# The conv projection as seven products of blocks, with its sums on VectorE

## The chip, the cores and the metric

The kernel runs on one NeuronCore of a Trainium2 chip. Its time is device microseconds of one execution; of several executions the median is taken. The engines of the core are TensorE (PE; its weight loads are listed apart as PEld), VectorE (DVE), ScalarE (ACT), GpSimd (POOL) and SyncE (SP), which issues most of the DMA transfers.

## The reference

One decoder layer on x of 1024 tokens x 1024 channels, float32. What matters here is the middle of it:

```python
a = rms_norm(a, subln_w[l]) * (1.0 - lam_init)
y_a = a.reshape(B, S, ATTN_WIDTH) @ w_proj_attn[l]

u_a, u_b = jnp.split(u, 2, axis=-1)
c = causal_depthwise_conv(u_a * jax.nn.sigmoid(u_b), conv_w[l], conv_b[l])
c = jax.nn.silu(layer_norm(c, conv_ln_w[l], conv_ln_b[l]))
y_b = c @ w_proj_conv[l]

g_a, g_b = jnp.split(jax.nn.sigmoid(g + gate_b[l]), 2, axis=-1)
x = x + (g_a * y_a + g_b * y_b) @ w_out[l]

h = rms_norm(x, ffn_norm_w[l])
gt, up = jnp.split(h @ w_gate_up[l], 2, axis=-1)
x = x + (jax.nn.silu(gt) * up) @ w_down[l]
```

All matrices of the middle part are 1024 x 1024. Below, c is the normed conv branch, m the gated sum g_a * y_a + g_b * y_b.

## The kernel before

Every large product is made of float32r matmuls. An operand is split into a part hi (a cast on ACT, split_hi, line 119) and a rest lo (a subtraction on DVE, split_lo, line 124), and mm3 (line 152) adds hi·hi, hi·lo and lo·hi into one PSUM bank, so that each product of 128 x 128 by 128 x 512 is three matmuls.

The stages follow one another: the input projection, interleaved with the conv taps and the attention of eight heads; then the attention projection y_a, the conv projection y_b, the output projection, and the feed-forward part. Up to the attention projection TensorE's operand is h, transposed, in two SBUF tiles of 128 x 8 x 1024 (hT_hi and hT_lo, tags xhi and xlo of the pool "big"). The same two places then hold cT_hi and cT_lo, then h2_hi and h2_lo, so that each waits until the one before it has been read for the last time.

**Attention projection** (lines 1486 to 1506). Two column blocks of w_proj_attn run together, then six one by one; each is 2 token halves x 8 k x 3 matmuls into two banks. ya_out loads the gate (gated, line 1469: a DMA and a Tanh on ACT, tag gt, four tiles), multiplies on DVE (gate_twice) and stores y_a's gated part in DRAM (ya_d). Beside it runs the conv branch's layer norm, as a generator per token half (ln_chunks, line 1396) that is advanced in steps given by two lists (lines 1450 and 1458): the rows of c are loaded into the place of cT_lo; the mean comes from a matmul with the sum over channels; the differences d are squared on ACT and added on DVE; then each row is scaled, goes through Silu, and is split into cT_hi and cT_lo.

**Conv projection** (lines 1508 to 1536). Eight column blocks in groups of three, two, two and one; for each group both token halves; each is gemm_T (line 375), 8 k x 3 matmuls into one bank. Then DVE multiplies with the gate and adds the reloaded y_a part, which gives a half row of m. Three quarters of m are split for TensorE. block_sums (line 1512) makes four sums of the blocks of m on DVE and stores them in DRAM (mso).

**Output projection** (lines 1628 to 1662). It is already done as seven products of 512 x 512 blocks (Winograd's form of Strassen's method): the list WO (line 446) names for each product a block or a sum of blocks of m ("12", "S1"), a block or a sum of w_out ("T2", made early and kept in DRAM), the group of four PSUM banks into which it is added ("a", "b", "c"), and the block of the result that is read out of them after it. s_load (line 1595) reloads a sum of m from mso, and splits it. Group b lies in the pool pw, the others in the pool ps. The rows of x are loaded into tiles xa, whose room is that of the gate tiles of the stage before (pool b1, closed at line 1537). In the last product the second norm begins (norm2, line 1571), whose transposes go through banks of ps (tr_first, line 1588).

Weights come through a Stream (line 342) that loads and splits two ahead of the one that is used: 512 KB each into one of two tiles wraw, split into one of three pairs whi and wlo. What a queue's instructions follow each other in is set by a planner that simulates the program; in_order (line 205) and after (line 127) fix some orders by hand.

## Time and profile before

| what | us |
|---|---|
| median of three executions | 1740.07 |
| lowest and highest | 1739.8, 1740.08 |
| the profiled execution's own time | 1738.13 |
| its span, first to last instruction | 1736.3 |
| attention projection, from and to | 835 to 927 |
| conv projection | 927 to 1014 |
| output projection | 1014 to 1095 |

The span is what the profile covers; the execution's own time has 1.8 us more around it. Stages are given by the first matmuls of each, in us from the start of the span. In the rows of groups, a line gives the source line, the engine, the operation, the tile written and the tiles read, the count, and then busy time and mean duration, and the idle time of the engine before these instructions with what ended it. A matmul's duration in such a row is not its price: the next one starts before it ends.

### The profile page before, as it was taken

The numbers are of one execution on the slowest core, as the hardware profiler recorded it, in microseconds if no ns is written. First come the engines' busy times: TensorE is split into PE (matmuls) and PEld (weight loads), VectorE is DVE, ScalarE is ACT, GpSimd is POOL, SyncE is SP. The second block draws the span as 40 slices with busy tenths as digits, with TensorE's granted clock in tenths as the row PEclk, the third lists the DMA queues.
The fourth block names the chain that finished last, engine by engine and source line by source line (L and its number), as shares of the span: only waits on it lengthen the run. The fifth ranks groups of instructions, "written<-read, shape, count | busy, mean of one in ns | idle before, by whom it ended". The sixth has DMA issues, their size and how long they took to land.

```text
span 1736.3 us, 25111 instructions
## 1 busy us (share of the span) xinstructions
PE 1726.8 (99%) x8954; PEld 1471.5 (85%) x8954; DVE 1292.2 (74%) x2202; ACT 794.8 (46%) x1873; POOL 27.1 (2%) x101
## 2 busy tenths in 40 slices
PE   9999999999999999999999999999999999999999
PEld 6878898999999998988888888888888888888887
DVE  8689988989889898885675567976676666565554
ACT  6121141667767776754564234633333333333332
POOL 0010000000000000000000000000000000000000
PEclk9999999999999999999999999999999999999999
DMA  7269545244444345364874677235445444697663
GB/s 244 91 201 305 183 124 136 71 120 131 122 142 114 89 120 151 87 173 139 288 245 134 200 246 251 86 107 178 152 159 172 158 149 152 224 352 241 218 216 131
DMA packets 260537, 295.22 MB, mean 170 GB/s; under 512 B 17730, under 2 KB 167283, under 8 KB 260412
## 3 DMA queue, kind: packets, MB, share of 16 engines
q1 hardware_dynamic: 257676, 283.73, 50.8%
q0 software_dynamic: 2432, 9.10, 2.2%
q8 instruction: 70, 1.15, 0.3%
q10 hardware_dynamic: 304, 0.79, 0.1%
q14 instruction: 55, 0.45, 0.1%
HBM read 189.19 MB, written 90.21 MB: 161 GB/s over the span
## 4 chain that ended last, share of the span: by engine, by line
PE 95%; DVE 2%; ACT 1%; DMA 1%; issue 0%; SPq 0%; DVEq 0%
PE acc L1819 22%; PE pg L153 14%; PE pg L154 14%; PE pg L155 14%; PE acc L532 12%; PE pg L737 4%; PE wo L1641 3%; PE sc L1152 2%; PE sc L1151 2%; PE pT L1187 2%; PE pW L155 1%; PE pW L153 1%; PE pW L154 1%; PE pQ L821 1%; DMA xa<-in_x_dram 0%; PE tr L1579 0%
## 5 line engine op out<-in xcount | busy, mean ns | idle before, releaser
L610 DVE SCALAR_TENSOR_TENSOR acc<-u,cw,acc 128x1024 f32<-128x1024 f32 x240 | 306.9, 1279 | 2.6
L153 PE MATMUL pg<-hT_hi,whi 128*128 128x512 f32 x512 | 201.5, 394 | 1.2 <-ACT sgg L646 0.9
L154 PE MATMUL pg<-hT_lo,whi 128*128 128x512 f32 x512 | 201.1, 393 | 0.0
L155 PE MATMUL pg<-hT_hi,wlo 128*128 128x512 f32 x512 | 200.8, 392 | 0.0
L120 ACT CAST whi<-wraw 128x1024 fp32r<-128x1024 f32 x101 | 106.3, 1052 | 149.0 <-PE pg L154 96.4
L125 DVE TENSOR_TENSOR wlo<-draw,whi 128x1024 fp32r<-128x1024 f32 x75 | 91.8, 1224 | 89.1 <-ACT whi L120 81.5
L125 DVE TENSOR_TENSOR wlo<-wraw,whi 128x1024 fp32r<-128x1024 f32 x102 | 124.3, 1219 | 44.7 <-ACT whi L120 41.4
L153 PE MATMUL pg<-whi,hT_hi 128*128 128x256 f32 x512 | 146.1, 285 | 0.3 <-ACT jk L805 0.3
L154 PE MATMUL pg<-wlo,hT_hi 128*128 128x256 f32 x512 | 145.7, 285 | 0.0
L155 PE MATMUL pg<-whi,hT_lo 128*128 128x256 f32 x512 | 145.3, 284 | 0.0
L120 ACT CAST whi<-draw 128x1024 fp32r<-128x1024 f32 x75 | 79.1, 1055 | 129.5 <-PE acc L532 119.3
L532 PE MATMUL acc<-wlo,whi 128*128 128x512 f32 x308 | 119.8, 389 | 0.0
L532 PE MATMUL acc<-whi,wlo 128*128 128x512 f32 x308 | 119.8, 389 | 0.0
L153 PEld LDWEIGHTS pg<-hT_hi,whi 128*128 128x128 f32 x512 | 96.2, 188 | 21.3 <-ACT sgg L646 1.7
L154 PEld LDWEIGHTS pg<-hT_lo,whi 128*128 128x128 f32 x512 | 96.2, 188 | 19.4 <-issue 0.6
L155 PEld LDWEIGHTS pg<-hT_hi,wlo 128*128 128x128 f32 x512 | 96.2, 188 | 19.2
L1158 ACT ACTIVATE E<-E,mn 128x256 f32<-128x256 f32 (+7 forms) x128 | 99.4, 778 | 28.2 <-DVE mn L1153 27.9
L153 PEld LDWEIGHTS pg<-whi,hT_hi 128*128 128x128 f32 x512 | 97.6, 191 | 1.9 <-ACT jk L805 0.5
L154 PEld LDWEIGHTS pg<-wlo,hT_hi 128*128 128x128 f32 x512 | 97.6, 191 | 1.5
L155 PEld LDWEIGHTS pg<-whi,hT_lo 128*128 128x128 f32 x512 | 97.6, 191 | 0.7
L1819 PE MATMUL acc<-h_hi,whi 128*128 128x512 f32 x240 | 93.4, 389 | 0.0
L1819 PE MATMUL acc<-h_lo,whi 128*128 128x512 f32 x240 | 93.4, 389 | 0.0
(321 smaller groups left out, 4182.2 us busy)
## 6 DMA issues: line engine op xcount, KB each, us to landing
wraw<-in_w_gate_up_dram SPq DMA_DIRECT2D x44, 512.0 KB, 4.6
wraw<-in_w_in_dram SPq DMA_DIRECT2D x37, 512.0 KB, 5.4
qs<-qs SPq DMA_DIRECT2D x96, 128.0 KB, 2.3
wd<-in_w_down_dram SPq DMA_DIRECT2D x44, 256.0 KB, 3.2
tdT<-wd SPq DMA_DIRECT2D x88, 128.0 KB, 4.2
draw<-sdS SPq DMA_DIRECT2D x44, 256.0 KB
draw<-tdT SPq DMA_DIRECT2D x44, 256.0 KB, 4.3
wraw<-in_w_in_dram SPq DMA_DIRECT2D x32, 256.0 KB, 4.6
```

The costliest lines, as they stand in the source:

```text
L120: act.copy(dst, src)
L125: last_lo[0] = dve.tensor_tensor(dst, src, f32(hi), op=ALU.subtract).ins
L153: pe.matmul(o, lh, rh, start=start, stop=False)
L154: pe.matmul(o, lh, rl, start=False, stop=False)
L155: last_mm[0] = pe.matmul(o, ll, rh, start=False, stop=stop).ins
L532: m = pe.matmul(o[s_][i][:], l_[:, ts], r_[:, 512:], start=start and j + y_ == 0, stop=j == n - 1 and y_ == 2, skip_group_check=not start,)
L610: dve.scalar_tensor_tensor(acc[0][:], us[c][:, t : t + S], cw[:, c, t : t + 1], acc[0][:], op0=ALU.mult, op1=ALU.add)
L737: last_mm[0] = pe.matmul(o[:], l_, r_, start=first and n_ == 0, stop=last and n_ == len(terms) - 1).ins
L1151: pe.matmul(o[:, :w], qh[:, qs], k, start=True, stop=False)
L1158: act.activation(e[:, :nk], e[:, :nk], AF.Exp, bias=mn[:, j : j + 1], scale=-1.0, accum_out=l[:, j : j + 1])
L1641: last_mm[0] = pe.matmul(o[s_][i][:], l_, r_[:, k, :], start=start and g + k + y_ == 0, stop=g == 1 and k == 1 and y_ == 2, skip_group_che ...
L1819: pe.matmul(o[:], a_[x_][:, k, :], b_[y_][:, k, :], start=start and k + x_ + y_ == 0, stop=k == 3 and x_ == 1, skip_group_check=not start,)
```

## The change

The conv projection is done in the way of the output projection: seven products of 512 x 512 blocks, transposed. The stationary operands are blocks and sums of blocks of w_proj_conv (YO's first entry), the moving ones blocks of c and sums of them (T1 to T4).

- side_weights makes S1 to S4 of the weights in four pieces, during the attention projection's third to sixth column block, and stores them in DRAM (wps). ld_side loads a block or such a sum.
- The layer norm stores the finished rows of the first token half in DRAM too (z_d). In the second half, four rows at a time (channel blocks j and j + 4 of both token halves) give the four sums; t_split splits them into tiles that take the places of aT, once the attention projection has read these.
- The tiles of h, c, and of the second norm are cut into quarters (class Quad: channel half and token half), each a tile with its own tag.
- The seven products' partial results are kept in SBUF (part_) or added to PSUM; m's quarters are kept in SBUF (mf, in places of c), and m's sums are made there and split in place. mso and s_load are gone.
- The output projection takes S1 second; its group b is now in ps and group c in pw, and the transposes of the second norm go through pw.

The diff, cut to its core:

```diff
+class Quad:
+    def __init__(self, pool, name, tag, halves=None):
+        self.t = {
+            q: pool.tile([P, NKT // 2, 512], F32R, tag=f"{tag}{q[0]}{q[1]}", name=f"{name}{q[0]}{q[1]}")
+            for q in (halves or ((0, 0), (1, 0), (0, 1), (1, 1)))
+        }
...
-    hT_hi = big.tile([P, NKT, S], F32R, tag="xhi", name="hT_hi")
-    hT_lo = big.tile([P, NKT, S], F32R, tag="xlo", name="hT_lo")
+    hT_hi = Quad(big, "hT_hi", "xh")
+    hT_lo = Quad(big, "hT_lo", "xl")
...
-    mso = {z: [dr.tile([P, 512], F32, name=f"mso{z}_{j}") for j in range(4)] for z in ("S1", "S2", "S3", "S4")}
+    wps = {z: [dr.tile([P, 512], F32, name=f"wps{z}_{j}") for j in range(4)] for z in ("S1", "S2", "S3", "S4")}
+    z_d = [dr.tile([P, 512], F32, name=f"z_d{c}") for c in range(NKT)]
...
     WO = (
         ("12", (1, 0), "a", (0, 0), False),
+        ("S1", "T1", "c", (1, 1), False),
         ("11", (0, 0), "b", (0, 0), True),
         ("S2", "T2", "b", (0, 1), False),
-        ("S1", "T1", "c", (1, 1), False),
         ("S4", (1, 1), "c", (0, 1), True),
         ("S3", "T3", "b", (1, 1), True),
         ("22", "T4", "b", (1, 0), True),
     )
+    YO = (
+        ("12", (1, 0), "a", (((0, 0), False),)),
+        ("11", (0, 0), "b", (((0, 0), True),)),
+        ("S4", (1, 1), "c", (((0, 1), False),)),
+        ("S2", "T2", "b", (((0, 1), False),)),
+        ("S1", "T1", "d", (((1, 1), False), ((0, 1), True))),
+        ("S3", "T3", "b", (((1, 1), True),)),
+        ("22", "T4", "b", (((1, 0), True),)),
+    )
+    def ld_side(a_, g):
+        def go():
+            raw = wraw()
+            r4 = raw[:].rearrange("p (q k c) -> p q k c", k=4, c=P)
+            for q in range(2):
+                j = 2 * g + q
+                if a_ in wps:
+                    nc.sync.dma_start(raw[:, 512 * q : 512 * (q + 1)], wps[a_][j][:])
+                else:
+                    c, e = 2 * j + 2 - int(a_[0]), int(a_[1]) - 1
+                    nc.sync.dma_start(
+                        r4[:, q], wpc[512 * e : 512 * (e + 1), c * P : (c + 1) * P].rearrange("(k p) c -> p k c", p=P)
+                    )
+            return [t_[:].rearrange("p (q k c) -> p q k c", k=4, c=P) for t_ in wsplit(raw)]
...
+    ws.plan([ld_side(a_, g) for a_, _, _, _ in YO for g in range(2)])
...
-    cT_hi = big.tile([P, NKT, S], F32R, tag="xhi", name="cT_hi")
-    cT_lo = big.tile([P, NKT, S], F32R, tag="xlo", name="cT_lo")
+    cT_hi = Quad(big, "cT_hi", "xh", ((0, 0), (1, 0), (1, 1)))
+    cT_lo = Quad(big, "cT_lo", "xl")
+    LNR = []
+    TOK = (slice(0, 512), slice(512, 1024))
+    TK = {"T2": (1, 3), "T1": (5, 7), "T3": (0, 2), "T4": (4, 6)}
+    TC = {}
+    def t_split(j, sums_):
+        for z, t_ in sums_.items():
+            hi, lo = [d_[TK[z][j // 2]][:, TOK[j % 2]] for d_ in TC[z]]
+            split_hi(hi, t_[:])
+            split_lo(lo, t_[:], hi)
...
+        if sb:
+            room = big.tile([P, 4, 512], F32, tag="xh01", name="ln_d")
+            LNR.append(room)
         for c in range(NKT):
             q = half("sq") if c else s2
-            d = half("csg" if sb == 0 and c % 2 else "d")
-            dve.tensor_tensor(d[:], cc[c], mean[:], op=ALU.subtract)
-            act.activation(q[:], d[:], AF.Square)
-            nc.sync.dma_start(cc[c], d[:])
+            d = room[:, c % 4, :] if sb else half("csg" if c % 2 else "d")[:]
+            dve.tensor_tensor(d, cc[c], mean[:], op=ALU.subtract)
+            act.activation(q[:], d, AF.Square)
+            nc.sync.dma_start(cc[c], d)
...
+        act.copy(LNR[0][:, 1 - sb, :], rb_[:])
...
+        for c in range(0 if sb else NKT):
+            nc.sync.dma_start(z_d[c][:], end(c, ("z", "sq", "csg", "d")[c % 4])[:])
             if c % 2:
                 yield
+        made = []
+        for j in range(4 if sb else 0):
+            while j == 2 and not TC:
+                yield
+            if j == 2:
+                for m_ in made:
+                    t_split(*m_)
+            t1, t4 = half("csg"), half("d")
+            nc.sync.dma_start(t1[:], z_d[j][:])
+            nc.sync.dma_start(t4[:], z_d[j + 4][:])
+            t3, t2 = end(j, "z"), end(j + 4, "sq")
+            dve.tensor_tensor(t1[:], t3[:], t1[:], op=ALU.subtract)
+            dve.tensor_tensor(t3[:], t2[:], t3[:], op=ALU.subtract)
+            dve.tensor_tensor(t2[:], t2[:], t1[:], op=ALU.subtract)
+            dve.tensor_tensor(t4[:], t4[:], t2[:], op=ALU.subtract)
+            made.append((j, {"T2": t2, "T1": t1, "T3": t3, "T4": t4}))
+            if j > 1:
+                t_split(*made[-1])
+            yield
...
-        for z in (0, 1, 0, 0, 0, 1, 1, 0, 0, 0, 0, 0, 1, 1, 1, 1, 1, 1):
+        for z in (0, 1, 0, 0, 0, 1, 1, 1, 0, 1, 0, 0, 0, 0, 1, 1):
...
-    lnp = [2, 2, 1, 2, 1, 2, 3, 1, 2, 9]
+    lnp = [2, 2, 1, 3, 2, 2, 2, 1, 1, 9]
...
+    def side_weights(j):
+        a = {}
+        for i in range(2):
+            for e in range(2):
+                a[i, e] = bp.tile([P, 512], F32, tag="ya", name=nm("sw"), bufs=4)
+                c = 2 * j + 1 - i
+                nc.sync.dma_start(
+                    a[i, e][:].rearrange("p (k c) -> p k c", c=P),
+                    wpc[512 * e : 512 * (e + 1), c * P : (c + 1) * P].rearrange("(k p) c -> p k c", p=P),
+                )
+        (a11, a12), (a21, a22) = [[a[i, e][:] for e in range(2)] for i in range(2)]
+        dve.tensor_tensor(a22, a21, a22, op=ALU.add)
+        dve.tensor_tensor(a21, a11, a21, op=ALU.subtract)
+        dve.tensor_tensor(a11, a22, a11, op=ALU.subtract)
+        dve.tensor_tensor(a12, a12, a11, op=ALU.subtract)
+        for z, t_ in (("S2", a11), ("S1", a22), ("S4", a12), ("S3", a21)):
+            nc.sync.dma_start(wps[z][j][:], t_)
...
+        if c < NE + 4:
+            side_weights(c - NE)
...
-    def block_sums(j):
...
+    for z in TK:
+        TC[z] = y_tiles(z, TK[z])
+    for _ in lnq:
+        pass
...
+    MF = {(0, 0): "xh10", (0, 1): "xl10", (1, 1): "xh00", (1, 0): "xl00"}
...
+    def m_out(i, l, j, src, g, ya):
+        gate_twice(src, g[:])
+        if (i, l) not in mf:
+            mf[i, l] = big.tile([P, 4, 512], F32, tag=MF[i, l], name=f"mf{i}{l}")
+        dve.tensor_tensor(mf[i, l][:, j, :], g[:], ya[:], op=ALU.add)
...
+    def term(j, k, w, b_, start):
+        bh, bl = c_part(b_, k)
+        for y_, (l_, r_) in enumerate(((w[0], bh), (w[0], bl), (w[1], bh))):
+            last_mm[0] = pe.matmul(
+                ob_[0][j][:], l_[:, j % 2, k, :], r_, start=start and k + y_ == 0, stop=k == 3 and y_ == 2,
+                skip_group_check=not start,
+            ).ins
+    for z, (a_, b_, s_, outs) in enumerate(YO):
...
+            wide = z in (2, 3)
+            w2 = [ws.next() for _ in range(2)] if wide else []
+            for g in range(2):
+                whi, wlo = w2[g] if wide else ws.next()
+                loads = {j: m_loads(*outs[-1][0], j) for j in (2 * g, 2 * g + 1)} if outs[-1][1] else {}
+                if wide and g == 0:
+                    for k in range(4):
+                        for j in range(4):
+                            term(j, k, w2[j // 2], b_, start)
+                for q in range(2):
+                    j = 2 * g + q
+                    ob = o[s_][j]
+                    for k in range(0 if wide else 4):
+                        term(j, k, (whi, wlo), b_, start)
+                    for (i, l), full in outs:
+                        src = ob[:]
+                        if (i, l, j) in part_:
+                            src = part_[i, l, j]
+                            dve.tensor_tensor(src, ob[:], src, op=ALU.add)
+                        elif not full:
+                            part_[i, l, j] = part_room(i, l, j)
+                            act.copy(part_[i, l, j], ob[:])
+                        if full and z == 1:
+                            late.append((i, l, j, src, *loads[j]))
+                        elif full:
+                            m_out(i, l, j, src, *loads[j])
+                        if full and z == 5:
+                            f1 = mf[0, 1][:, j, :]
+                            m_split(0, 1, j)
+                            dve.tensor_tensor(f1, mf[1, 1][:, j, :], f1, op=ALU.add)
+        if z == 3:
+            for m_ in late:
+                m_out(*m_)
+        if z == 4:
+            for j in range(4):
+                m_split(0, 0, j)
+        if z == 5:
+            s_room("S1", ("xh11", "xl11"))
+            for j in range(4):
+                s_split("S1", j)
+    s_room("S2", ("xh01", "xl01"))
+    for j in range(4):
+        m_split(1, 0, j)
+    for j in range(4):
+        a11, a12, a21, s1 = [mf[q][:, j, :] for q in ((1, 0), (0, 0), (1, 1), (0, 1))]
+        dve.tensor_tensor(a21, a11, a21, op=ALU.subtract)
+        dve.tensor_tensor(a11, s1, a11, op=ALU.subtract)
+        s_split("S2", j)
+        dve.tensor_tensor(a12, a12, a11, op=ALU.subtract)
+    SP_["S4"] = lambda j: (mT_hi[2 * j][:, TOK[1]], mT_lo[2 * j][:, TOK[1]])
+    for j in range(4):
+        s_split("S4", j)
+    s_room("S3", ("xl00", "xl10"))
+    for j in range(4):
+        s_split("S3", j)
...
-    def s_load(z):
...
+        (0, 0): lambda: x_rows(0, 0), (0, 1): lambda: x_rows(1, 1), (1, 1): lambda: x_rows(0, 1),
+        (2, 1): norm_weights, (3, 1): lambda: x_rows(1, 0),
...
-            o[s_] = [(pw if s_ == "b" else ps).tile([P, 512], F32, tag="pw" if s_ == "b" else PS_TAGS[i], name=nm("wo")) for i in range(4)]
+            o[s_] = [(pw if s_ == "c" else ps).tile([P, 512], F32, tag="pw" if s_ == "c" else PS_TAGS[i], name=nm("wo")) for i in range(4)]
```

More of the change, by code (lines that the diff above doesn't have):

```diff
@@ L389, in gemm_N @@
             whi, wlo = halves[k // 4]
[L390 removed]
+            mm3(o, kt(shi, k, ts), kt(slo, k, ts), whi[:, k % 4, :], wlo[:, k % 4, :], k == 0, k == NKT - 1)
     v_hi = [dr.tile([S, 512], F32, name=f"v_hi{j}") for j in range(2)]
@@ new lines, with s_room, part_room @@
+    SF = {"S1": (0, 1), "S2": (1, 0), "S4": (0, 0), "S3": (1, 1)}
+    def s_room(z, tags):
+        hi, lo = [big.tile([P, 4, 512], F32R, tag=t_, name=f"{z}{t_}") for t_ in tags]
+        SP_[z] = lambda j: (hi[:, j, :], lo[:, j, :])
+    PTAG = {(0, 0): ("s", "s", "sg", "sg"), (1, 1): ("z", "z", "csg", "csg")}
+    o, part_ = {}, {}
+    def part_room(i, l, j):
+        if (i, l) == (0, 1) and j:
+            return LNR[0][:, j, :]
+        tag = PTAG[i, l][j] if (i, l) in PTAG else "s"
+        return (wp if tag == "sg" else bp).tile([P, 512], F32, tag=tag, name=nm("yp"), bufs=2)[:]
@@ new lines, in term @@
+    def term(j, k, w, b_, start):
[5 more added lines that the diff above has]
+            ).ins
+    ob_, late = [None], []
+    for z, (a_, b_, s_, outs) in enumerate(YO):
+        start = s_ not in o
+        if start:
+            o[s_] = [
+                pln.tile([P, 512], F32, tag=("mean", "rstd")[j - 2], name=nm("yo"), bufs=1) if s_ == "b" and j > 1
+                else (py if s_ == "b" else ps).tile([P, 512], F32, tag="pg4" if s_ == "b" else ("pm", "pg")[j // 2], name=nm("yo"))
+                for j in range(4)
+            ]
+        ob_[0] = o[s_]
+        with in_order(mybir.EngineType.PE):
+            wide = z in (2, 3)
[38 more added lines that the diff above has]
+                s_split("S1", j)
@@ L1774, in wd_tiles @@
         return [b[:, 0], b[:, 1]]
-    KH = (slice(0, 4), slice(4, 8))
-    B = {(j, l): (h2_hi[:, KH[j], TOK[l]], h2_lo[:, KH[j], TOK[l]]) for j in range(2) for l in range(2)}
+    B = {(j, l): (h2_hi.half(j, TOK[l]), h2_lo.half(j, TOK[l])) for j in range(2) for l in range(2)}
     def prepare(f):
```

116 lines of the change are left out of this document (53 added, 63 removed).

## The prediction

> **What bounds the kernel now.** First the page: span, busy time by engine, the clock that was granted, and the chain that ended last.
>
> ```profile
> span 1736.3 us, 25111 instructions
> ...
> PE 1726.8 (99%) x8954; PEld 1471.5 (85%) x8954; DVE 1292.2 (74%) x2202; ACT 794.8 (46%) x1873; POOL 27.1 (2%) x101
> ...
> PEclk9999999999999999999999999999999999999999
> ...
> PE 95%; DVE 2%; ACT 1%; DMA 1%; issue 0%; SPq 0%; DVEq 0%
> ```
>
> TensorE is busy all along at full clock, and the chain runs through it: a matmul less is time less, as long as the others keep feeding it. The changed stage must show the same. The table by stretches takes the attention projection (835 to 927), then the conv projection (to 1014); the tile query gives the products that read cT_hi.
>
> ```profile
> 835.00:881.00 46.00, 46.00 (x204) 37.45 (x203) 30.06 (x55) 21.53 (x32) 0.00 (x0) 1.00 0.99 350
> 881.00:927.00 46.00, 46.00 (x212) 38.18 (x211) 31.11 (x58) 28.38 (x42) 0.00 (x0) 1.00 0.58 188
> 927.00:957.00 30.00, 30.00 (x134) 24.86 (x133) 18.82 (x28) 14.45 (x21) 0.00 (x0) 1.00 0.41 124
> 957.00:986.00 29.00, 29.00 (x129) 24.01 (x129) 17.96 (x26) 7.86 (x11) 0.00 (x0) 1.00 0.70 222
> 986.00:1014.00 28.00, 28.00 (x125) 23.17 (x125) 14.34 (x20) 6.49 (x9) 0.00 (x0) 1.00 0.43 147
> ```
>
> ```profile
> L153 PE MATMUL pg<-cT_hi,whi x128: 389/389/389, 927.1 to 1013.5; 128*128 128x512 f32 x128
> L155 PE MATMUL pg<-cT_hi,wlo x128: 389/389/389, 927.6 to 1013.9; 128*128 128x512 f32 x128
> L120 ACT CAST cT_hi<-lnz x16: 601/612/622, 889.2 to 936.8; 128x512 fp32r<-128x512 f32 x16
> ```
>
> Columns of the stretches: length, busy us of PE, PEld, DVE, ACT and POOL, clock, DMA share, GB/s. TensorE has no gap in either stage. The reader must not take the 389 ns for the price of a matmul: they overlap. With line 154's there are 384 of them, first start 927.1, last 1013.9: 86.8 us over 383 steps is **226.6 ns** each.
>
> **The change part by part.**
>
> *Products.* Before: 8 column blocks x 2 token halves x 8 k x 3 = 384. After: 7 block products x 4 j x 4 k x 3 = 336, of the same form, each with its own weight load as now. 48 x 226.6 ns = **10.9 us off**; the stage takes 76.2 us and one block product 10.9 us.
>
> [...]
>
> *The seam to the output projection.* The two waits are all that TensorE has between 780 and 1110; below them is the chain at the second one.
>
> ```profile
> PE pW L153 <- DVE pl L125: 0.9, 1, 0.9
> PE wo L1641 <- DVE xa L1654: 0.6, 1, 0.6
> ```
>
> ```profile
> 1019.95 5.47 DMA msoS<-ya
> ...
> 1026.33 7.13 DMA xa<-in_x_dram
> ...
> 1036.68 3.44 PE wo L1641 x14
> ```
>
> The rows of x are loaded into the room of the gate tiles, whose last user is the store of m's sums to DRAM, so they come late. After the change m's sums stay in SBUF: the 16 stores (mso) and the 16 reloads of s_load go, the room is free after the last gate's addition, and the two blocks that share a bank set have S1's product between them. I take **0.6 us off**. What is late next is S1's split, priced below.
>
> *DVE.* One 512-wide operation and one weight split cost, in the conv stage:
>
> ```profile
> L1477 DVE SCALAR_TENSOR_TENSOR gt<-gt,pg 128x512 f32<-128x512 f32 x16 | 11.0, 686 | 23.5 <-PE pg L155 23.5
> L125 DVE TENSOR_TENSOR wlo<-wraw,whi 128x1024 fp32r<-128x1024 f32 x8 | 9.7, 1218 | 0.0
> ```
>
> Attention stage: now 30.1 + 31.1 = 61.2 us busy of 92. Added: 16 sums of weights, 8 of the norm's rows; two splits move out. 22 x 0.686 = 15.1; 76.3 of 92 fits.
> Conv stage: due before TensorE reaches S1's product in the output projection, 76.2 + 10.9 = 87.1 us after the start, are 30 operations of the norm's end (4 scalings, 8 sums, 18 splits), 16 additions of partial blocks, 24 of gates (three quarters of m), 8 splits of m, S1's 4 sums and 4 splits: 86 x 0.686 = 59.0. With 16 weight splits (14 of this stage and 4 of the next, 2 done early) x 1.218 = 19.5 that is **78.5 us of 87.1**, where now 18.8 + 18.0 + 14.3 = 51.1 are busy. 8.6 us are spare: covered, but this is the thinnest cover. The last quarter of m and the other sums (36 operations, 24.7 us) are due 11 to 44 us later, beside the output projection, which loses 16 splits of reloaded sums.
>
> *The waits added.* The splits of the norm's sums (t_split) need the rooms of aT, so they start at the end of the attention stage, 927. T2's are first read after three block products, 32.7 us later. Until then two of four rows need 8 + 8 splits at once, then z_d's reload, scaling and sums, some 20 us with both engines taking turns (16 x 0.686 = 11.0 on DVE, the rest chained). Behind them on DVE wait the weight splits of the next products, and TensorE behind those. ACT adds 32 casts and copies of 0.612 and 6 weight casts, at most 1.05 us each: 28.8 busy becomes 55 of 76. Covered.
>
> *DMA.* Here the cover is thin too.
>
> ```profile
> 830.00:835.00 5.00, 5.00 (x28) 4.24 (x27) 4.63 (x6) 2.93 (x5) 0.21 (x1) 1.00 0.14 53
> ...
> 845.00:850.00 5.00, 5.00 (x22) 3.77 (x21) 2.78 (x5) 1.78 (x3) 0.00 (x0) 1.00 1.05 401
> ```
>
> ```profile
> DMA packets 7752, 8.64 MB, mean 188 GB/s; under 512 B 471, under 2 KB 4567, under 8 KB 7750
> ...
> wraw<-in_w_proj_conv_dram SPq DMA_DIRECT2D x4, 512.0 KB, 5.0
> ...
> ya<-ya_d SPq DMA_DIRECT2D x2, 256.0 KB
> ```
>
> ```profile
> ya<-ya_d SPq DMA_DIRECT2D x4, 256.0 KB, 5.2
> ```
>
> Full engines move 401 GB/s. The second fence is 881 to 927: its four weight loads are 2.1 MB in pieces of 512 B; the other 6.5 MB take 16.3 us at 401, which leaves 10.4 of 0.58 x 46 = 26.7 us for them: about 202 GB/s. The attention stage uses 0.99 x 46 + 26.7 = 72.2 us. Added: side_weights' 16 loads of 256 KB in such pieces, 4.19 MB at 202, 20.7 us; its 16 stores 10.5; 8 stores and 4 reloads of the norm's rows 7.8. Six early loads of ya (4 + 2 in the two halves, the last fence being 835 to 881) go, 3.9. **107.3 us of work in 92.** Something gives:
>
> ```profile
> 835.38 0.32 SPq L1407 DMA_DIRECT2D cT_lo<-c_d  x1
> ```
>
> The norm's rows load only when all of hT is free; in quarters, the first half comes free one 512-token block earlier, and 2.4 MB, 5.9 us, move into a stretch with share 0.14. The other 9.4 us can slip past 927, into a stage that uses 45 of its 87 us, if what slips isn't awaited: ya_d's stores and the sums of weights (S4's are read some 11 us in) can wait, gate loads and weights can't. All go through SP, where 44 more issues stand, of 0.32 us or more each; a side_weights load that waits for its room holds the weights behind it.
>
> *New waits of TensorE*: no row shows them; from 0 to 9.4 us. I take **1.5**, all that it waits in the rows above, since weights and norm are ready well ahead by these accounts.
>
> Sum: -10.9 - 0.6 + 1.5 = -10.0. The profiled execution took 1738.13 (1.8 around its span of 1736.3): 1728.1. The median stands 1.94 above it, 1740.07: **1730.0**.
>
> **The rivals.**
>
> *DMA takes the gain back.* The 9.4 us that don't fit fall on TensorE: gates' loads sit behind 1 MB of side weights, at 5.2 us each, and a product's PSUM bank isn't freed. 1740.07 - 11.5 + 9.4 = 1738.0 at worst, 1733 to 1738 in part. For it: share 0.99 and more where these loads go. Against: weights are loaded two ahead, 22 us, and gate tiles are four deep; share 0.99 cost TensorE nothing. [...]
>
> *DVE becomes the bound (slower).* Place: between S2's product and S1's split. DVE takes its queue in order; if it idles in this stage as now, 87.0 - 51.1 = 35.9 us, it ends 35.9 - 8.6 = 27.3 late and TensorE waits for it: 1740.07 - 11.5 + 27.3 = 1755.9. It decides from 8.6 us of idle on; from 8.6 + 11.5 = 20.1 the kernel is slower. For it: gate loads follow the release of four tiles, S1's product sends out two blocks at once, ACT and DVE alternate. Against: of the idle now, 23.5 us is DVE waiting for products, having nothing else to do; it will have.
>
> **How the numbers follow.** A measurement of this kernel tells 0.2%, 3.5 us, from no change: 1736.6 to 1743.5. Forecast 0.62, 1727.5 (waits 0, and 1 us for the seam's second wait and the spread) to 1733. DMA 0.20, of it 0.13 under 1736.6. DVE 0.18, of it 0.14 over 1743.5 and 0.04 between. Faster 0.75, same 0.11, slower 0.14. The range goes to 1739, the end of the DMA rival with 1 us for the spread; the DVE rival is left out.
>
> **What would show it.** Products: 336 rows at starts 226.6 ns apart. Seam: no wait for xa, no mso rows. Waits of TensorE, by releaser: gt, wlo or whi in 835 to 927 means DMA; wlo, T or S1 splits from 960 on mean DVE, whose busy time between would be near 90%. I am wrong if the stage's start moves by more than 2 us against 927, or if TensorE waits over 3 us in one place.

## The result, and the profile after

The changed kernel takes 1728.92 us in the median (1727.65 to 1729.44 in four executions). The kernel before took 1739.93 in the same session; the ratio is 0.9938 with a 95% interval of 0.9926 to 0.9951, so it is faster by 0.5 to 0.7%. The profiled execution took 1727.65 us, 10.48 less than that of before. The forecast was 1730.0.

The page of the changed kernel: span, busy time by engine, granted clock, and the chain that ended last.

```profile
span 1725.9 us, 25202 instructions
...
PE 1715.8 (99%) x8906; PEld 1462.6 (85%) x8906; DVE 1330.0 (77%) x2268; ACT 812.1 (47%) x1905; POOL 27.1 (2%) x101
...
PEclk9999999999999999999999999999999999999999
...
PE 91%; DVE 4%; DMA 2%; ACT 2%; issue 1%; SPq 0%; DVEq 0%; ACTq 0%
```

TensorE has 48 matmuls less and is as full as before. DVE has 66 instructions and 37.8 us more. The chain now passes through DVE for 4% of the span where it was 2%: DVE is nearer to being the limit, without being it. The table by stretches, with the columns of the prediction's table:

```profile
835.00:881.00 46.00, 46.00 (x205) 37.47 (x204) 35.13 (x58) 22.96 (x36) 0.08 (x1) 1.00 1.05 369
881.00:927.00 46.00, 46.00 (x212) 38.21 (x211) 38.48 (x79) 28.30 (x44) 0.00 (x0) 1.00 0.94 324
927.00:957.00 30.00, 29.87 (x133) 24.38 (x132) 28.74 (x45) 18.31 (x29) 0.00 (x0) 1.00 0.67 222
957.00:986.00 29.00, 29.00 (x130) 24.01 (x129) 21.85 (x31) 16.92 (x26) 0.00 (x0) 1.00 0.66 210
986.00:1003.50 17.50, 17.50 (x79) 14.50 (x78) 17.50 (x28) 7.70 (x12) 0.00 (x0) 1.00 0.71 237
```

The second number of each row is TensorE's busy time: 0.13 us are missing in one row, none in the others. Compare the fourth number, DVE: 73.6 us of the 92 of the attention stage, where it had been 61.2, and all 17.5 us of the last part of the conv stage. The share of the DMA engines in 881 to 927 has gone from 0.58 to 0.94. The tile query gives the new products (yo).

```profile
L1675 PE MATMUL yo<-cT_hi,whi x48: 387/389/396, 927.3 to 959.7; 128*128 128x512 f32 x48
L1675 PE MATMUL yo<-T4h,wlo x16: 389/389/389, 993.5 to 1003.7; 128*128 128x512 f32 x16
```

And all waits of TensorE from 780 to 1110:

```profile
PE pW L171 <- DVE pl L143: 0.9, 1, 0.9
```

That wait lies in the attention and was there before; the wait for xa is gone. Where the time went, by the first matmuls of each stage in the two traces:

| stretch | before | after | difference |
|---|---|---|---|
| up to the conv projection | 927.1 | 927.3 | +0.2 |
| conv projection | 87.06 | 76.60 | -10.46 |
| output projection | 80.60 | 79.73 | -0.87 |
| feed-forward part, to the end of the span | 641.54 | 642.27 | +0.73 |
| span | 1736.3 | 1725.9 | -10.4 |

The conv stage could have been 336 x 0.2266 = 76.14 us. The rest is one stutter at 951.16, in the product S4, where two matmuls start 0.52 and 0.33 us behind the one before: 0.4 us over the usual step, at a split of the low weights that ends just then.

### The profile page after: what moved, and what is told of

Same layout as the page of the kernel before. It is cut to its first block, busy times and chain, and to the rows that moved or that the text cites. A ratio compares the mean times of both kernels' runs of the same rounds, so it can differ in the third digit from the quotient of the medians.

```text
span 1725.9 us, 25202 instructions
## 1 busy us (share of the span) xinstructions
PE 1715.8 (99%) x8906; PEld 1462.6 (85%) x8906; DVE 1330.0 (77%) x2268; ACT 812.1 (47%) x1905; POOL 27.1 (2%) x101
## 4 chain that ended last, share of the span: by engine, by line
PE 91%; DVE 4%; DMA 2%; ACT 2%; issue 1%; SPq 0%; DVEq 0%; ACTq 0%
PE acc L2009 20%; PE acc L578 12%; PE pg L171 12%; PE pg L172 12%; PE pg L173 12%; PE wo L1832 4%; PE pg L783 4%; PE yo L1675 3%; PE sc L1198 2%; PE sc L1197 2%; PE pT L1233 2%; PE pW L171 1%; PE pW L173 1%; PE pW L172 1%; PE pQ L867 1%
## 5 line engine op out<-in xcount | busy, mean ns | idle before, releaser
L138 ACT CAST whi<-wraw 128x1024 fp32r<-128x1024 f32 x107 | 112.7, 1053 | 161.2 <-PE pg L172 89.5
L143 DVE TENSOR_TENSOR wlo<-wraw,whi 128x1024 fp32r<-128x1024 f32 x108 | 131.5, 1217 | 39.7 <-ACT whi L138 39.5
```

Of the source, the lines that this page charges most:

```text
L138: act.copy(dst, src)
L143: last_lo[0] = dve.tensor_tensor(dst, src, f32(hi), op=ALU.subtract).ins
```

## The experiments

All are edits of the changed kernel. Times are medians; ratios are to the kernel before, timed on the same chip beside them. The changed kernel's own ratio is 0.9938.

| edit | us | ratio, 95% interval |
|---|---|---|
| one block product twice | 1739.56 | 1.0003 (0.9994 to 1.0012) |
| no sums of weights | 1737.01 | 0.9988 (0.9979 to 0.9997) |
| output projection in the old order | 1734.39 | 0.9974 (0.9964 to 0.9983) |
| 24 more DVE steps, S1 and S3 | 1745.48 | 1.0033 (1.0020 to 1.0046) |
| 8 more DVE steps, S1 and S3 | 1732.52 | 0.9959 (0.9946 to 0.9973) |
| 8 more DVE steps, S1 only | 1732.76 | 0.9966 (0.9954 to 0.9979) |
| 16 more DVE steps, attention projection | 1730.59 | 0.9953 (0.9936 to 0.9969) |
| weights for sums in 2 KB pieces | 1728.15 | 0.9940 (0.9926 to 0.9954) |
| halves of the norm's rows exchanged | 1728.84 | 0.9939 (0.9926 to 0.9953) |
| norm's rows loaded late | 1730.03 | 0.9951 (0.9936 to 0.9966) |
| all products with one loop order | 1727.94 | 0.9934 (0.9922 to 0.9946) |
| pauses of TensorE, one execution | 1843.4 | |

The theory at the start: the gain is the 48 matmuls, TensorE sets the time, and DVE is the thinnest cover. The rivals: full DMA engines keep part of the gain, or something other than the matmuls made it.

### One product twice

```diff
-                    for k in range(0 if wide else 4):
-                        term(j, k, (whi, wlo), b_, start)
+                    for _ in range(2 if z == 0 else 1):
+                        for k in range(0 if wide else 4):
+                            term(j, k, (whi, wlo), b_, start)
```

> The changed kernel, with its first block product of the conv projection (12) issued twice into the same banks, the second time overwriting: 48 matmuls more, nothing else. Theory (the gain is the 48 matmuls that went, at 226.6 ns each, and the others keep pace with TensorE): 10.9 us more, 1739.8, the time of before. Rival (VectorE or the DMA engines set the end of this stage, TensorE only waits less than before): the added matmuls fall into their time, less than 5 us more, under 1734.

Measured 1739.56 us, 10.6 over the changed kernel. The tile query of this run:

```profile
L1675 PE MATMUL yo<-cT_hi,whi x64: 388/390/390, 928.6 to 971.4; 128*128 128x512 f32 x64
```

T2's product starts at 972.1: 43.5 us for four block products, where the changed kernel takes 960.4 - 927.3 = 33.1 for three. One block product is 10.4 us, or 10.8 without the changed kernel's stutter. That is the theory's price, and far from the rival's "less than 5 us": the price of a matmul in this stage is the step between starts (48 x 0.2266 = 10.9 us), and no hidden slack stands behind it.

### The sums of weights left out

```diff
-        if c < NE + 4:
-            side_weights(c - NE)
```

> The changed kernel without the sums of w_proj_conv's blocks: their loads, 16 VectorE sums and 16 stores are left out, and the four products that read sums load plain blocks. Theory (the attention stage's DMA engines are full, 1.05 and 0.94 of their time, but nothing that TensorE waits for is late): within 0.7 us of the changed kernel, 1728.2 to 1729.6, although the DMA share of 881 to 927 falls by a third or more. Rival (full DMA engines cost part of the gain): 2 us or more faster, under 1727.

Measured 1737.01 us: less work on DVE and the DMA engines, and 8 us slower. Both theories missed. The waits of TensorE from 780 to 1110 in this run:

```profile
PE yo L1672 <- DVE wlo L143: 4.4, 3, 3.7
PE yo L1672 <- ACT whi L138: 1.2, 1, 1.2
```

and ACT's timeline (start, duration, then in brackets the idle time before it and what ended it):

```profile
928.66 0.63 ACT L1558 ACTIVATE gt<-gt 128x512 f32<-128x512 f32 x1 [5.36 <-DMA gt<-g_d]
...
961.66 0.63 ACT L1558 ACTIVATE gt<-gt 128x512 f32<-128x512 f32 x1 [7.05 <-DMA gt<-g_d]
```

Without the sums the planner orders every queue anew. ACT now stands at a gate whose load is late, and other casts stand behind it in its queue; DVE's splits wait for the casts, and TensorE for the splits. DVE's first split behind the gate at 928.66:

```profile
929.83 1.29 DVE L143 TENSOR_TENSOR T3l<-lnz,T3h 128x512 fp32r<-128x512 f32 x2 [6.00 <-ACT T3h L138]
```

The chain to TensorE's wait of 3.7 us runs through this gate's load (4.27 us) and then through the reload of a row of the norm (4.15 us), for which DVE's queue stands. Behind the gate at 961.66 and one more late gate stands the cast of weights for which TensorE waits 1.2 us. So this run doesn't measure the sums; it shows what a wait at the head of a queue cost here: 5.36 and 7.05 us of ACT's time, 3.7 and 1.2 of TensorE's. Loading as many bytes for the sums in another way (below) leaves the order of the queues nearly as it is.

### The output projection in its old order

```diff
-        ("S1", "T1", "c", (1, 1), False),
         ("11", (0, 0), "b", (0, 0), True),
         ("S2", "T2", "b", (0, 1), False),
+        ("S1", "T1", "c", (1, 1), False),
```

The banks, and the order in which rows of x are loaded, go back with it.

> The changed kernel with the output projection in its old order (S1 fourth), with the old bank groups and the old order of x's rows. Theory (VectorE's queue runs some microseconds behind; the block product 11 needs the splits of m's last quarter, which in the changed kernel end at 1026.4, and would now be read from 1014.8 on): TensorE waits 5 to 11 us in the second product, 1734 to 1740. Rival (the order matters little, since the planner puts the due splits first): under 2 us more, under 1731.

Measured 1734.39 us, 5.5 over the changed kernel. Waits of TensorE, then its timeline behind the long one:

```profile
PE wo L1835 <- DVE xa L1848: 2.5, 1, 2.5
...
PE wo L1835 <- DVE mTl L143: 0.5, 1, 0.5
```

```profile
1029.97 0.69 PE L1835 MATMUL wo<-whi,S2xh 128*128 128x512 f32 x1 [2.52 <-DVE xa L1848]
1030.45 0.63 PE L1835 MATMUL wo<-wlo,S2xh 128*128 128x512 f32 x1
1030.88 0.63 PE L1835 MATMUL wo<-whi,S2xl 128*128 128x512 f32 x1
```

The time is in the theory's range, but the place is not: the splits of m's last quarter (mTl) cost 0.5 us of the 5 to 11 expected. A wait at the seam is back, and larger than the 0.6 of before, although m's sums stay in SBUF. It isn't the same wait: before the change the chain to it ran through the load of xa, and here, from 1010 to 1035, it holds no DMA transfer:

```profile
by line: PE wo L1835 20.3%; issue 14.2%; DVE xa L1848 13.4%; DVE wlo L143 9.2%; DVE mTl L143 8.2%; DVE mf L1737 7.8%; DVE S2xl L143 7.5%; DVE S1xl L143 5.5%; DVE mf L1739 5.1%; DVE mf L1649 4.8%; DVE mf L1736 4.8%; DVE gt L1564 0.3%
```

DVE's queue is what is late. So the changed kernel needs the new order, with the banks and rows that belong to it (the three were put back together); whether the stores' going alone would have removed the old 0.6 us isn't shown. The run also shows something the prediction had no term for. Behind the wait the matmuls start 0.43 us apart, nine of them, instead of 0.227; that costs 1.8 us more.

### More steps for DVE

```diff
                             m_out(i, l, j, src, *loads[j])
+                        for _ in range(3 if full and z in (4, 5) else 0):
+                            f_ = mf[i, l][:, j, :]
+                            dve.tensor_tensor(f_, f_, f_, op=ALU.max)
```

> The changed kernel with 24 more VectorE operations of 128x512 (the maximum of a row of m with itself, which changes nothing), three behind each of the eight gates of the products S1 and S3: 24 x 0.60 us from start to start is 14.4 us. Theory (the cover on VectorE is thin: S1's last split ends at 1012.5 and is read at 1020.2, the last quarter's splits at 1026.4 and are read from 1025.7 to 1031): some 5 to 8 us are hidden, TensorE waits for the rest, 6 to 10 us, 1735 to 1739. Rival (VectorE has the room that its idle share suggests): under 3 us more, under 1732.

Measured 1745.48 us, 16.6 more for 14.4 us of work; both expectations were too low. TensorE's waits:

```profile
PE wo L1835 <- DVE S1xl L143: 6.7, 2, 4.7
PE wo L1835 <- ACT S1xh L138: 5.0, 1, 5.0
```

That is 11.6 us of waits, all for S1's sums, and matmuls 0.42 or 0.43 us apart behind them. From this I took the cover to be 14.4 - 11.6 = 2.8 us, and tried a third of the steps (1 in place of 3).

> Eight extra VectorE steps (the maximum of a 512-wide row of m with itself, one behind each of the eight gates of the products S1 and S3), 8 x 0.60 = 4.8 us by the rows of such steps, a third of those in the run with 24 of them, which cost 16.6 us. Theory A (the cover in the convolution's last products is only about 2.8 us thick: in the run with 24, 14.4 us of work gave waits of 11.6 us on S1's sums): about 2 us of waits on S1's sums, 1730.0 to 1732.5 us. Theory B (the prediction's cover of 8.6 us holds for work that is spread evenly, and the 24 lost more than their own length because the order of the queues went wrong there): no wait on S1's sums over 0.5 us and a time of 1728.2 to 1729.6 us. A time over 1733 us would say that the cover is nil and that the steps cost more than their length.

Measured 1732.52 us, 3.6 over the changed kernel for 4.8 us of work; the upper end of theory A. But its waits don't bear out the reason: only one is for S1.

```profile
PE wo L1835 <- DVE S1xl L143: 1.1, 1, 1.1
PE wo L1835 <- ACT mTh L138: 1.1, 1, 1.1
PE wo L1835 <- DVE xa L1848: 0.6, 1, 0.6
```

The splits of S1's sums, by the tile query, in the changed kernel and in the run with eight steps (first and last start):

```profile
L143 DVE TENSOR_TENSOR S1xl<-mf,S1xh x4: 676/677/678, 999.3 to 1011.8; 128x512 fp32r<-128x512 f32 x4
```

```profile
L143 DVE TENSOR_TENSOR S1xl<-mf,S1xh x4: 673/674/675, 1009.8 to 1021.7; 128x512 fp32r<-128x512 f32 x4
```

4.8 us of work put the last split 9.9 us later, since the order of DVE's queue has eight added and six other operations ahead of it. In the changed kernel it ends at 1012.5, and TensorE first reads it at 1021.35 (the last of the four k): 8.9 us of cover, not 2.8. If that were all, eight steps that push nothing else ahead of the split should cost nothing. So the eight were put behind S1's gates alone, two each:

```diff
+                        for _ in range(2 if full and z == 4 else 0):
```

> Eight extra VectorE steps again (4.8 us), but all behind the four gates of the product S1, two each, with which the order of VectorE's queue puts no other work ahead of S1's last split: it stands seven places later than in the changed kernel, where in the run with eight steps spread over S1 and S3 it stood fourteen places later (the eight and six others) and ended 9.9 us later. Theory A (the last split of S1's sums ends 8.9 us before it is read, so that 4.8 us are hidden and the former run lost its time by the new order): no wait on S1's splits over 0.3 us, 1728 to 1730 us. Theory B (there is no spare time on VectorE there, and any step of it costs TensorE most of its length): 1731 to 1734 us.

Measured 1732.76 us. There is no wait for S1, as theory A has it, and the time is that of theory B. TensorE's waits, with the split's row:

```profile
PE wo L1835 <- DVE xa L1848: 3.3, 3, 1.3
```

```profile
L143 DVE TENSOR_TENSOR S1xl<-mf,S1xh x4: 681/682/685, 1007.9 to 1018.6; 128x512 fp32r<-128x512 f32 x4
```

The loss has moved to the next dates in DVE's queue, the additions to xa that empty the output projection's banks. From 1024 to 1044 DVE is busy for 20.00 of 20 us in this run. Transfers are late as well: the rows of x start to load at 1018.86, behind additions of gates, where in the changed kernel they start at 1015.1, and the chain to the last of these waits runs through one such load of 5.93 us. Why the loss moves on is seen in the changed kernel's table, from the last gap before S1's sums to the third gap after it:

```profile
979.00:1022.78 43.78, 43.78 (x195) 36.26 (x194) 42.89 (x65) 23.85 (x36) 0.00 (x0) 1.00 0.64 211
1022.78:1043.27 20.49, 20.49 (x92) 16.98 (x91) 19.64 (x30) 10.55 (x19) 0.00 (x0) 1.00 0.77 258
```

In these 64.27 us DVE is idle for 0.89 + 0.85 = 1.74 us. Whatever is added in front comes out at one date or another; a single date, such as S1's split, can have 8.9 us of cover and the queue next to none. Before 979 there is more: 18.4 us of the attention stage and 8.3 of the conv stage are idle. Sixteen steps there, 9.6 us:

```diff
             gate_twice(os2[sb][:], g[:])
+            dve.tensor_tensor(g[:], g[:], g[:], op=ALU.max)
```

> Sixteen extra VectorE steps of 0.60 us (the maximum of a gated tile with itself, 9.6 us in all) in the second half of the attention stage, one behind each gate of its output, where VectorE is busy 73.6 of 92 us. Theory A (the cover is thin only where VectorE is busy without a gap, from about 986 us on; in the attention stage 18 us are idle): within 1 us of the changed kernel, 1728 to 1730 us, no wait of TensorE over 1 us. Theory B (the work of the attention stage is followed by the convolution's without a break, so that what is late here is late at S1's sums as well): 9.6 us less what is idle on the way, 2 us or more of waits in the convolution or behind it, 1731 to 1736 us.

Measured 1730.59 us, between the theories: 1.7 over the changed kernel (by the ratios 0.0015, or 2.6), where steps later on cost three quarters or more of their length. The wait is for weights:

```profile
PE yo L1676 <- DVE wlo L143: 1.0, 1, 1.0
```

The intervals of the two ratios overlap. The sixteen steps also gave DVE's queue a new order, and the chain to this wait runs through the reload of a row of ya (3.75 us) that stands ahead of the split: the 1.7 us are not the price of DVE's time alone.

### The DMA engines

First the blocks for the sums in longer pieces, on the same queues:

```diff
-                    a[i, e][:].rearrange("p (k c) -> p k c", c=P),
-                    wpc[512 * e : 512 * (e + 1), c * P : (c + 1) * P].rearrange("(k p) c -> p k c", p=P),
+                    a[i, e][:],
+                    wpc[c * P : (c + 1) * P, 512 * e : 512 * (e + 1)],
```

> The blocks of the convolution's projection weights for the side sums are loaded as 128 rows of 2 KB in place of 512 pieces of 512 bytes: as many bytes, the same instructions on every other engine in the same order. What is loaded so are other elements of the weights, so the sums, and with them the output, are not the reference's. Theory A (the DMA engines, busy for 1.05 and 0.94 of the two halves of the last 92 us of the attention, hold nobody up there): within 0.7 us of the changed kernel, 1728.2 to 1729.6 us, with about 10 us less DMA busy time between 835 and 927. Theory B (full DMA engines still cost the changed kernel part of its gain, by late weights or rows): 1 us or more faster, under 1727.9 us.

Measured 1728.15 us, not told apart from the changed kernel. But the DMA engines are hardly less busy either. From 835 to 927 in the changed kernel and in this run (next to last column):

```profile
835.00:927.00 92.00, 92.00 (x415) 75.68 (x414) 73.61 (x136) 51.25 (x80) 0.08 (x1) 1.00 1.00 347
```

```profile
835.00:927.00 92.00, 92.00 (x415) 75.67 (x414) 74.51 (x137) 51.06 (x80) 0.16 (x1) 1.00 0.98 353
```

0.02 x 92 = 1.8 us less, where the prediction's 202 GB/s for pieces of 512 B against 401 would give 10. The run also moves 6 GB/s more, 0.55 MB in the 92 us, which is 1.4 us at 401 GB/s. So that price was too high: the 4.19 MB of blocks cost some 2 to 3 us more in short pieces, not 10.

Then the norm's rows, which the change loads early.

```diff
-    hT_hi = Quad(big, "hT_hi", "xh")
+    hT_hi = Quad(big, "hT_hi", "xh", turned=1)
```

> The quarters of the transposed input sit in the other token half's memory, so the norm's rows that are loaded over them come free later, as before the change, and about 2.4 MB (5.9 us of all DMA engines at the 401 GB/s that the trace shows) no longer move ahead of 835 us. Theory A (this early load is what lets 107 us of DMA work pass in a stage of 92 us): the rows or the gates' reloads slip 4 to 8 us into the convolution, TensorE waits 2 us or more there, 1731 to 1738 us. Theory B (what slips past 927 us are writes and reads that are wanted only late): no wait over 1 us, 1728.2 to 1729.9 us.

Measured 1728.84 us, but the edit didn't do what it was for: the planner exchanged the two halves of rows as well, and the first of them was still issued at 827.25 us. It shows only that it doesn't matter which half comes first. With the second half's rows tied behind the first's:

```diff
+        with after(first_rows[0] if sb else None):
+            for c in range(NKT):
+                nc.sync.dma_start(cc[c], c_d[c][:, cs])
```

> The norm's rows of the first token half now load over the quarters of h that are read last, and those of the second half are issued behind them, so that the loads wait as before the change (from about 832 to 835 us, not 826.5); the run before it had only exchanged the halves, and its rows still loaded from 827.3 us. Theory A (what does not fit into the 92 us of full DMA engines slips into the convolution and waits there for nobody): within 1 us of the changed kernel, 1728 to 1730 us, no wait of TensorE over 1 us in the convolution, but a higher DMA share from 927 to 945. Theory B (the changed kernel keeps its gain only because some 2.4 MB, 5.9 us, move ahead of 835 us): waits of 2 to 6 us at late gates or weights and slow matmuls behind them, 1731 to 1737 us.

SyncE's timeline in the changed kernel and in this run:

```profile
826.53 1.76 SPq L1464 DMA_DIRECT2D cT_lo<-c_d  x4
```

```profile
832.73 1.27 SPq L1467 DMA_DIRECT2D cT_lo<-c_d  x3
```

The rows are 6.2 us later. How much DMA time that moves is read from the share in the 15 us up to 835, in the kernel before, the changed kernel and this run:

```profile
820.00:835.00 15.00, 15.00 (x73) 12.48 (x72) 8.91 (x13) 9.33 (x18) 0.21 (x1) 1.00 0.21 70
```

```profile
820.00:835.00 15.00, 15.00 (x73) 12.49 (x72) 8.88 (x12) 9.13 (x17) 0.13 (x1) 1.00 0.49 166
```

```profile
820.00:835.00 15.00, 15.00 (x70) 12.37 (x70) 8.31 (x12) 8.60 (x16) 0.00 (x0) 1.00 0.24 75
```

The change moved 0.28 x 15 = 4.2 us ahead of 835, 1.4 MB and not the 2.4 expected, and this run takes 0.25 x 15 = 3.8 us of it back. Measured 1730.03 us, 1.1 over the changed kernel (2.3 by the ratios, whose intervals overlap), with waits of 0.9 and 0.5 us for weights at T2's product. What slips is seen in the share of the DMA engines from 927 on, first in the changed kernel:

```profile
927.00:935.00 8.00, 8.00 (x38) 6.60 (x36) 8.00 (x15) 6.65 (x12) 0.00 (x0) 1.00 0.86 278
```

```profile
927.00:935.00 8.00, 8.00 (x37) 6.64 (x36) 8.00 (x13) 8.00 (x13) 0.00 (x0) 1.00 0.98 331
```

So the early load is worth at most 1 to 2 us, less than the DMA time that it moves: most of what slips is awaited by nobody. The two waits stand behind a gate's load of 4.7 us at the head of ACT's queue, which has a new order here as well, so they can't be put down to the late rows alone.

### One loop order for all products

```diff
-            wide = z in (2, 3)
+            wide = False
```

> All seven products run with the input blocks in the outer loop; S4 and S2 of the changed kernel run with the output rows' order turned so that the low weights are needed later. Theory A (by the changed kernel's trace the low weights of S4 end at 951, within the product; with the other order their second quarter is wanted earlier or later by under 2 us): 1728.2 to 1729.7 us, and only small waits on the low weights, at most 1 us in all. Theory B (the wide order is what covers VectorE's split of the weights there): waits of 2 us or more on the low weights at S4 or S2, and 1731 us or later, with a stretch of matmuls 0.42 us apart behind them.

Measured 1727.94 us; the stutter at 951 is gone and no wait takes its place. Its ratio can't be told from the changed kernel's, so it isn't claimed as the better version, though it is simpler.

### What a pause of TensorE costs

```diff
+        if f in PAUSE:
+            held = sm.tile([P, 16], F32, tag="r", name=nm("held"))
+            dve.tensor_copy(held[:], b[:, :16])
+            for _ in range(PAUSE[f]):
+                dve.tensor_scalar(held[:], held[:], 0.5, None, op0=ALU.mult)
+            dve.tensor_copy(a[:, :16], held[:])
         product(a, A["12"], B[1, 0], True)
```

> Twenty pauses of TensorE in the feed-forward stage: in twenty pairs VectorE takes a narrow 128x16 copy of the first product's bank, works n steps on it one behind the other (n from 1 to 22, each length twice) and writes it into the next product's bank, which TensorE then overwrites; within these pairs TensorE keeps the order of the program, so nothing fills the pause. The pauses should be some 0.5 to 4 us long. Theory A (a short pause costs its length, a pause from about 2 us on is followed by matmuls 0.42 to 0.43 us apart for 3 to 5 us, as behind the waits of the runs before): behind the pauses under about 1.5 us the steps are 0.23 us at once, behind those over 2.5 us 8 to 17 steps of 0.42 us follow, 1.6 to 3.4 us more each. Theory B (the slow stretches of those runs were due to something else in that stage, late operands or the memory, and not to the pause): steps of 0.23 us behind all of the pauses.

The waits of TensorE, then its timeline at two of them:

```profile
PE acc L2009 <- DVE acc L2029: 76.2, 18, 6.7
PE acc L2009 <- DVE u L2045: 2.0, 1, 2.0
PE acc L2009 <- ACT u L2036: 1.2, 1, 1.2
```

```profile
1177.37 0.47 PE L2009 MATMUL acc<-h_hi,whi 128*128 128x512 f32 x1 [2.95 <-DVE acc L2029]
...
1199.12 0.50 PE L2009 MATMUL acc<-h_hi,whi 128*128 128x512 f32 x1 [2.44 <-DVE acc L2029]
...
1199.92 0.63 PE L2009 MATMUL acc<-h_hi,whi 128*128 128x512 f32 x1
1200.34 0.63 PE L2009 MATMUL acc<-h_lo,whi 128*128 128x512 f32 x1
```

Eighteen of the twenty pauses came about, as the feed-forward part has no pairs 22 and 23, and they were longer than meant, 2.44 to 6.7 us. Behind 17 of the 18 follow 6 to 12 matmuls 0.42 or 0.43 us apart, where the step is 0.227; the pause of 2.95 us, the first, has none, nor have the waits of 1.22 and 2.01. A slow stretch costs 1.5 to 2.5 us: 1.7 behind the second pause of 2.44 us, 1.6 behind one of 4.24. Behind the pauses of 2.44 us it starts 0.8 us after the matmuls resume, behind those of 3.28 us and more at once. Pauses and waits of 79.4 us and slow stretches of 31 make 110 of the 115.7 us by which this span is longer; the rest is left over. Theory A holds in kind, with 6 to 12 slow steps where it had 8 to 17. There was no pause under 2.44 us but the two waits.

So the length of a pause alone doesn't decide: 2.95 us escaped and 2.44 didn't. Behind the first pause of 2.44 us the matmuls were slow for 3.41 us (1199.92 to 1203.33). The next rows give slices of that length, with the granted clock third from the end: the two slices that the pause of 2.95 us lies in, then the slice of that pause of 2.44 us and the one behind it.

```profile
1172.60:1176.01 3.41, 1.82 (x9) 1.16 (x7) 3.41 (x8) 0.59 (x1) 0.00 (x0) 1.00 0.62 231
1176.01:1179.42 3.41, 2.05 (x9) 1.75 (x10) 1.58 (x6) 0.00 (x0) 0.00 (x0) 1.00 0.94 283
```

```profile
1196.49:1199.90 3.41, 0.97 (x4) 0.67 (x4) 2.50 (x10) 0.59 (x1) 0.00 (x0) 1.00 0.80 231
1199.90:1203.31 3.41, 3.41 (x9) 2.67 (x8) 0.00 (x0) 0.00 (x0) 0.00 (x0) 0.50 0.65 231
```

Around the longer pause the clock is 1.00 in both slices; behind the shorter one it is 0.50 for a slice. TensorE is busy for 1.82 and 2.05 us of the first two and for 0.97 us of the third. Which difference between the two pauses decides isn't shown.

## Why the prediction was right, step by step

**Products, -10.9: right.** The stage went from 87.06 to 76.60 us; the 0.4 us between that and 76.2 belong to the waits. One product twice gave the same price from the other side.

**Seam, -0.6: right in sign, a little small, its reason half tested.** Measured -0.87. The prediction named both the stores that go and S1's product in between. The old order brings a wait of 2.5 us without any such store, by a late DVE and not by late rows. So the order is needed; which of the two took away the old 0.6 us is open.

**DVE's cover: the busy time right, the 8.6 us met by luck, the conclusion too kind.** Busy in the attention stage 73.6 us for a predicted 76.3; in the conv stage up to the end of S1's last split 77.1 (the row below) for 78.5. Two errors cancel in that: the row has 115 operations where the prediction counted 102, and steps of 0.60 us where it took the duration, 0.686.

```profile
927.00:1012.49 85.49, 85.36 (x377) 70.34 (x376) 77.08 (x115) 48.88 (x75) 0.00 (x0) 1.00 0.66 216
```

The cover of 8.9 us isn't the predicted 8.6 either. The prediction counted to the start of S1's product and let DVE work without a gap. DVE was idle for 85.49 - 77.08 = 8.4 us on the way, so that only 2.3 us were left when that product started, at 1014.78; the last split is first read 6.6 us later.

What failed is the next step, that the 24.7 us of other work, due 11 to 44 us later, need no account of their own. They fill DVE up to 1043, so 4.8 us more there cost 3.6 and 3.8 (3.7 and 4.9 by the ratios). The rival "DVE becomes the bound" had the right engine and place, but the point wrong: the prediction let it decide from 8.6 us of idle time on. The changed kernel, with 8.4 and DVE busy for 90% as the rival's sign had it, waits for nothing there, and in both runs 4.8 us of added work were too much.

**Waits added by t_split: right, with less to spare.** T2's product began at 960.4, right behind the three products before it, with no wait. Its splits took 26 us instead of some 20:

```profile
L143 DVE TENSOR_TENSOR T2l<-lnsq,T2h x4: 675/680/683, 927.0 to 952.8; 128x512 fp32r<-128x512 f32 x4
```

**DMA, 107.3 us of work in 92: the term for the small pieces was mis-sized.** The side weights were put at 20.7 us; the long pieces save 2 to 3 us of the 10 that this price implies, so 7 to 8 us of the overflow of 9.4 were never there. The rows that moved ahead took 4.2 us with them, not 5.9. What slipped past 927 cost TensorE at most the stutter, as forecast. The 401 GB/s of 845 to 850 in the kernel before are those of loads from DRAM, which SyncE issues there and in the 6 us before:

```profile
844.15 6.04 SPq L1407 DMA_DIRECT2D cT_lo<-c_d  x8
```

**New waits, +1.5: measured 0.4**, the stutter. Not in the sum were 0.73 us behind the output projection and 0.2 before the stage. Their cause is open: they are within the spread between executions, and no experiment was made on them. The first product starts between 927.3 and 928.8 us in the profiles of the changed kernel and its edits.

**The price of a wait: missing in the rivals.** Both priced a wait of TensorE at its length. In the run with pauses 1.5 to 2.5 us came on top of 17 of the 18, which were 2.44 to 6.7 us long. Had either rival come true with waits of that length, it would by this have been dearer than forecast; the sum itself had no such wait.

In all: -10.46 - 0.87 + 0.73 + 0.2 = -10.4 for a predicted -10.0, with terms off by 0.3 to 1.1 us on both sides: that they nearly cancel is luck. The other 0.7 of the 1.1 us between forecast and median are no term of the change. The prediction added 1.94 us for the median over the profiled execution, and here it stands 1.27 above it.

## What to carry to other kernels

Where TensorE is busy all along, a matmul less is worth the step between starts (here 0.2266 us), as long as every engine that feeds it keeps its dates; so list all dates of a queue, and count the idle time in front of each, not in front of the first alone. An experiment that adds or removes instructions under a planner changes the order of all queues: look at the order before the time is read, or choose an edit that leaves it alone. And a wait of TensorE can cost more than its length: here it was 1.5 to 2.5 us more for 17 of the 18 pauses of 2.44 to 6.7 us.

## What the runs showed of the hardware that wasn't expected

- Behind 17 of 18 pauses of 2.44 to 6.7 us the matmuls started 0.42 or 0.43 us apart in place of 0.227, 6 to 12 of them, and not in the order of the pauses' lengths: 9 behind 2.44 us, 6 behind 4.12, 12 behind 5.40. Behind one of 2.44 us the granted clock was 0.50 for 3.41 us; the pause of 2.95 us had no such stretch behind it.
- Pieces of 512 B in place of 2 KB for 4.19 MB cost the DMA engines 2 to 3 us, not the 10 that a rate worked out from one stretch's share had given.
- DMA engines with a share of 1.05 and 0.94 over 92 us, and of 1.02 and 1.03 with the norm's rows late, went with waits of TensorE of 0 and 1.4 us behind them.
